# Modulation vectors of a convolution layer, partly from TensorE: eight tiles moved from VectorE into the convolution's last groups and a layer norm, with more room for banded matrices

## The chip, the cores and the metric

One core of a Trainium2 chip runs the whole program in one launch. The metric is device time in microseconds (us); the kernel before took 2941.39 us, the median of three runs (2937.71 to 2943.6). In the text PE is TensorE, DVE is VectorE, ACT is ScalarE, POOL is GpSimd and SP is the engine that issues most of the transfers.

## The reference

Two layers over 1024 latent tokens and 256 context tokens of width 1024. Layer 0 mixes tokens with a convolution module, layer 1 with grouped-query attention; each is followed by a SwiGLU FFN. Only layer 0's convolution matters here:

```python
mod_x = (silu_c @ w_mod[i] + b_mod[i])[:, None, :]
mod_c = silu_cc @ w_mod[i] + b_mod[i]
sh_x, sc_x, g_x, shf_x, scf_x, gf_x = jnp.split(mod_x, N_MOD, axis=-1)
...
u = h @ w_pw1 + b_pw1
a, gt = jnp.split(u, 2, axis=-1)
u = a * jax.nn.sigmoid(gt)
u = lax.conv_general_dilated(u, w_dw[:, None, :], ..., feature_group_count=u.shape[-1]) + b_dw
u = jax.nn.silu(layernorm(u, ln_g, ln_b))
return u @ w_pw2 + b_pw2
```

The modulation vectors are 6 x 1024 numbers for each of two conditions (latents and context). In the kernel they are 48 tiles of 128, with f the tile's number: tiles 0 to 15 are needed first, 16 to 23 scale the mixer's output, 24 to 39 are shift and scale of the FFN's norm, 40 to 47 scale its output.

## The kernel before

The 1280 tokens lie side by side in three pieces: the context C (256), the latents' first half L and second half R (512 each). The channels are on the partitions, eight tiles of 128.

**pw1** (lines 440 to 474) is a loop over k = 0 to 7. Each iteration multiplies two weight tiles (value and gate) with C, L and R in turn, each product in three matmuls (L454, L455, L456: high and low parts). It yields four times a piece, twelve times an iteration. At a piece's end ACT applies the gate's sigmoid (L462) and DVE multiplies (L463), which also empties the two PSUM banks; PE has three banks for pw1, so the third quarter of the next piece waits for that L463. After C's and R's L463 the result is loaded in another layout into U by transfers that SP and ACT issue in turn (L472). One iteration later ACT and DVE split U into a high and a low part (L161, L164).

**The convolution** runs as matmuls with banded matrices, in 64 groups (8 for each k). A group is ten matmuls (L532, L533, L535), ACT's eviction with bias (L536) and DVE's sum (L538). Three PSUM banks rotate, so a group needs the L538 of the group three before it. DVE builds a group's two banded matrices ("a map" is the pair, and each L506 makes one half of it) from a window of the weights (L164 of 320 columns prepares it). The maps lie in places that rotate: three in tile T6 at first; three in T1 and three in T2 are added in the last iteration, so nine. A place is free again when its group has run. The generator of the groups (`cg`) is advanced at the yields of pw1, two of three of them from the yield 22 on; at pw1's end 16 groups are left (48 to 63). After the eight groups of one k, DVE sums them over the channel (L565, L567). While the last eight run, `shift` centres the context's part ahead of its norm: L575 on DVE, L577 on PE, L594 on DVE.

**The modulation** of tiles 0 to 15 is made on PE in the prologue (`mod_pe`, L236 to L250). Tiles 16 to 39 are made on DVE during pw1 (`mod_dve`, L257 to L282): one multiply-and-sum instruction for each of the two conditions and tile (L273, and a short second instruction that reads the sum out), 48 in all, each tile's weights loaded ahead into one of two buffers in turn. The generator `modg` is advanced at two of three yields. The rest (40 to 47) is made later and isn't touched.

**After the groups** come the layer norms: `ln("C")` (L594 and L630 centre, L365 sums over channels, L370 and L343 to L351 compute the root, L379 spreads it, L643 and L646 apply), then `ln("L")`, `pw2("C")` (L665), `ln("R")`, `pw2("L")` and so on. `derive` (L319, L324) turns modulation vectors into columns. What R's norm reads (tile T5) is loaded from DRAM (L610) like C's and L's, piece by piece, as soon as the groups of a k are written.

Within what the buffers and the data allow, a scheduler orders each engine's instructions when the program is built; so where an instruction stands on its engine is not where the code calls it. The rows of that order are shown with the change. The names in them: HR holds the pw1 result and the groups' sums, KB holds U and raw windows, HS the split U, q the windows, T the maps, ps PSUM, cst constants, wr and wl weights.

Of the kernel before, what the change touches and what calls it, by code (L numbers as in the profile page):

```python
# [9 lines left out]
F32R = mybir.dt.float32r  # L10
# [5 lines left out]
P = 128  # L16
D = 1024
KT = D // P
# [20 lines left out]
NM = 5  # L39
# [16 lines left out]
class Kern:  # L56
# [454 lines left out]
    def conv(self):  # L511

        nc, c = self.nc, self.c
        for q in range(KT * CG):
            k, g = divmod(q, CG)
            u2, v = self.u2[k % 2], self.v[k == KT - 1]
            for _ in range(2):
# [1 line left out]
                    self.conv_maps()  # L519
            if q == CG * (KT - 1):  # L520
                self.cvs = {}
                for b, t in (("C", "KB"), ("L", "T4"), ("R", "T5")):
                    self.cvs[b] = self.T(t, [P, KT, PIECES[b][1] - PIECES[b][0]])
                    for j in range(KT - 1):
                        self.load_cv(b, j)
# [13 lines left out]
            if g == CG - 1:  # L539
# [6 lines left out]
                        eng.dma_start(d[k].rearrange("g q n -> q g n"), v[:, :, o0:o0 + nn])  # L546
                if k == KT - 1:
                    self.load_cv("L", k)
                    self.load_cv("R", k)

                self.conv_sum(v[:, CG - 2:] if k == KT - 1 else v, k)
            elif k == KT - 1:
# [638 lines left out]
    def build(self):  # L1191
        nc, a, c = self.nc, self.a, None
# [6 lines left out]
        cr = [hr[:, TOK + nv:TOK + nv + 1024], self.T("HV", [P, 1024])]  # L1199
# [64 lines left out]
        mraw = kt[:, CG * UW + nw:]  # L1264
        q = self.room()
        self.cwin = [q[:, o:o + nw].bitcast(F32R) for o in (0, 512)]
        cw = self.T("T6", [P, 6, NM * P], F32R)
        self.cw = [(cw[:, 2 * i], cw[:, 2 * i + 1]) for i in range(3)]
        self.cwq, self.cwi = [], 0
        for o, n in ((0, 2), (2 + NC_, 2), (UW - 2, 2)):  # L1270
            nc.gpsimd.memset(self.U[:, :, o:o + n], 0.0)
        modg = self.mod_dve(range(16, 40), cr, (mraw, None), self.ps[:, 5:7].rearrange("p a b -> p (a b)"))
        nc.vector.tensor_copy(self.craw[:, 0:1], hs["R"][0][1][:, KT - 1, 0:1].bitcast(F32))
        nc.sync.dma_start(self.craw, a["wwin"][0])
        self.conv_maps()
# [18 lines left out]
        self.banks["st"], self.ring["st"] = [6, 5], 0  # L1294
        for _ in range(4):
# [9 lines left out]
        self.set_banks(mm=[0, 1, 2, 3, 4, 7], st=[5, 6])  # L1305
# [61 lines left out]
        t = self.T("KB", [P, 2, 4, 256], F32R)  # L1367
# [356 lines left out]
```

## Time and profile before

| what | before |
| --- | --- |
| median of three runs | 2941.39 us (2937.71 to 2943.6) |
| the profiled execution, its own time | 2938.98 us |
| its span | 2937.2 us, mean granted PE clock 0.987 |
| prologue | 0 to 60 us |
| pw1 with groups 0 to 47 | 60 to 343 us |
| groups 48 to 63 | 343 to 374 us |
| the context's norm | 374 to 386 us |
| granted PE clock, 375 to 390 us | 0.59 |

Reading it: the page's first part gives each engine's busy time and share of the span. A row of the timeline gives start, duration, engine, line, operation, output and input names with their shapes, and in brackets the idle time before it and what ended it. A table of waits gives for each line what it waited for: us in total, how many times, and the longest. A row of stretches gives busy time and count of each engine, then the granted PE clock, the share of the transfer engines, and GB/s.

### The profile page before, as it was taken

How to read it: one execution, taken by the hardware profiler on the slowest of the kernel's cores; microseconds unless marked ns; L12 is line 12 of the kernel's file. 1: busy time of each engine (PE TensorE's matmuls, PEld its weight loads, DVE VectorE, ACT ScalarE, POOL GpSimd, SP SyncE). 2: the span in 40 equal slices, each digit the busy share in tenths (PEclk: the TensorE clock that was granted, in tenths of full speed). 3: DMA queues.
4: the chain of work that ended last, by engine and by line, in shares of the span. 5: the costliest groups of instructions: out<-in, count | busy, mean ns of one | idle time of the engine just before them, and what ended most of it. 6: DMA issues, size and time to landing. Idle time of an engine off the chain costs nothing.

```text
span 2937.2 us, 42731 instructions
## 1 busy us (share of the span) xinstructions
PE 2847.7 (97%) x16462; PEld 2446.1 (83%) x16462; DVE 2160.7 (74%) x3746; ACT 1335.5 (45%) x2229; POOL 222.6 (8%) x377
## 2 busy tenths in 40 slices
PE   7999989999999999999999999989999999999998
PEld 6888877888888889989888787767777778889997
DVE  6887788847556378877786899786666666786777
ACT  5222255532222245544445688645555543444444
POOL 0000001011022001000011111110000000010000
PEclk9999999999999999999999999999999999999999
DMA  6443444334356224333345211322222143353332
GB/s 249 140 120 98 116 131 145 135 116 143 115 175 198 65 74 165 114 104 112 109 156 170 88 46 46 97 87 81 66 73 83 60 149 99 110 170 104 102 98 75
DMA packets 131755, 336.58 MB, mean 115 GB/s; under 512 B 31328, under 2 KB 52864, under 8 KB 130656
## 3 DMA queue, kind: packets, MB, share of 16 engines
q1 hardware_dynamic: 78016, 222.33, 24.1%
q0 software_dynamic: 29344, 103.83, 10.7%
q10 hardware_dynamic: 24192, 7.70, 1.1%
q8 instruction: 129, 2.11, 0.3%
q14 instruction: 74, 0.61, 0.1%
HBM read 289.50 MB, written 38.93 MB: 112 GB/s over the span
## 4 chain that ended last, share of the span: by engine, by line
PE 86%; DVE 7%; ACT 2%; issue 2%; DMA 2%; ACTq 0%; POOL 0%; SPq 0%; DVEq 0%; POOLq 0%
PE ps L172 15%; PE ps L173 15%; PE ps L174 15%; PE ps L875 4%; PE ps L877 4%; PE ps L876 4%; PE ps L1116 4%; PE ps L1134 4%; PE ps L1140 2%; PE ps L454 2%; PE ps L455 2%; PE ps L456 2%; PE ps L1141 2%; PE ps L185 1%; PE ps L183 1%
## 5 line engine op out<-in xcount | busy, mean ns | idle before, releaser
L172 PE MATMUL ps<-T,wh 128*128 128x512 f32 (+1 forms) x1360 | 502.5, 370 | 1.4 <-ACT T L161 0.8
L174 PE MATMUL ps<-T,wl 128*128 128x512 f32 (+1 forms) x1360 | 500.4, 368 | 2.0 <-DVE wl L148 2.0
L173 PE MATMUL ps<-T,wh 128*128 128x512 f32 (+1 forms) x1312 | 481.4, 367 | 0.2 <-DVE T L164 0.2
L144 ACT CAST wh<-wr 128x1024 fp32r<-128x1024 f32 (+1 forms) x217 | 225.0, 1037 | 419.9 <-PE ps L173 307.2
L148 DVE TENSOR_TENSOR wl<-wr,wh 128x1024 fp32r<-128x1024 f32 (+1 forms) x217 | 261.9, 1207 | 168.5 <-ACT wh L144 167.1
L875 PE MATMUL ps<-T,wh 128*128 128x256 f32 x1092 | 310.7, 285 | 5.0 <-ACT wh L161 4.5
L876 PE MATMUL ps<-T,wh 128*128 128x256 f32 x1092 | 306.5, 281 | 0.0
L877 PE MATMUL ps<-T,wl 128*128 128x256 f32 x1092 | 305.4, 281 | 0.2 <-DVE wl L164 0.2
L1138 DVE TENSOR_TENSOR T<-ps,T 128x512 fp32r<-128x512 f32 x320 | 216.8, 687 | 107.6 <-ACT T L1137 106.8
L172 PEld LDWEIGHTS ps<-T,wh 128*128 128x128 f32 x1360 | 257.8, 190 | 43.7 <-ACT T L1506 1.7
L174 PEld LDWEIGHTS ps<-T,wl 128*128 128x128 f32 x1360 | 257.7, 190 | 42.4 <-DVE wl L148 2.2
L173 PEld LDWEIGHTS ps<-T,wh 128*128 128x128 f32 x1312 | 248.5, 189 | 38.2 <-DVE T L164 1.3
L1137 ACT CAST T<-ps 128x512 fp32r<-128x512 f32 x320 | 186.0, 586 | 191.1 <-PE ps L1134 177.6
L173 PE MATMUL ps<-HS,wh 128*128 128x512 f32 x656 | 257.9, 393 | 0.0
L172 PE MATMUL ps<-HS,wh 128*128 128x512 f32 x608 | 238.4, 392 | 0.9 <-ACT wh L144 0.9
L174 PE MATMUL ps<-HS,wl 128*128 128x512 f32 x608 | 237.5, 391 | 0.0
L875 PEld LDWEIGHTS ps<-T,wh 128*128 128x128 f32 x1092 | 206.1, 189 | 11.2 <-ACT wh L161 6.7
L876 PEld LDWEIGHTS ps<-T,wh 128*128 128x128 f32 x1092 | 206.6, 189 | 0.5
L877 PEld LDWEIGHTS ps<-T,wl 128*128 128x128 f32 x1092 | 206.2, 189 | 0.6 <-DVE wl L164 0.4
L1134 PE MATMUL ps<-cst,T 128*128 128x128 f32 x1100 | 189.6, 275 | 3.2 <-DVE T L1138 3.1
L1122 DVE TENSOR_SCALAR_CACHE_REDUCE T<-ps,rq 128x1280 f32<-128x1280 f32 x110 | 170.0, 1546 | 27.9 <-PE ps L1116 22.1
L1134 PEld LDWEIGHTS ps<-cst,T 128*128 128x128 f32 x1100 | 132.6, 141 | 49.5 <-DVE T L1138 30.8
(377 smaller groups left out, 6195.9 us busy)
## 6 DMA issues: line engine op xcount, KB each, us to landing
wr<-in_w SPq DMA_DIRECT2D x170, 512.0 KB, 3.6
wr<-in_pw SPq DMA_DIRECT2D x35, 512.0 KB, 3.5
HV<-in_wmodT POOLq DMA_DIRECT2D x56, 256.0 KB, 4.1
q<-in_wmodT POOLq DMA_DIRECT2D x56, 256.0 KB, 3.9
KB<-in_w SPq DMA_DIRECT2D x24, 512.0 KB, 3.6
HR<-in_w SPq DMA_DIRECT2D x23, 512.0 KB, 3.7
q<-in_w SPq DMA_DIRECT2D x23, 512.0 KB, 4.2
q<-qsd POOLq DMA_DIRECT2D x32, 256.0 KB, 3.3
```

Of the source, the lines that this page charges most:

```text
L144: nc.scalar.copy(hi, raw)
L148: nc.vector.tensor_tensor(lo, raw, hi.bitcast(F32), op=ALU.subtract)
L172: nc.tensor.matmul(out[:, :n], lhsT=wh, rhs=xh, start=k == 0, stop=False)
L173: nc.tensor.matmul(out[:, :n], lhsT=wh, rhs=xl, start=False, stop=False)
L174: nc.tensor.matmul(out[:, :n], lhsT=wl, rhs=xh, start=False, stop=k == nk - 1)
L875: nc.tensor.matmul(out, lhsT=wh, rhs=bh, start=first and k == 0, stop=False, **skip)
L876: nc.tensor.matmul(out, lhsT=wh, rhs=bl, start=False, stop=False, **skip)
L877: nc.tensor.matmul(out, lhsT=wl, rhs=bh, start=False, stop=k == 3, **skip)
L1122: nc.vector.tensor_scalar(out=pt, in0=sc, scalar1=rq[:, h:h + 1], scalar2=None, op0=ALU.mult, op1=ALU.min, accum_out=mn)
L1134: nc.tensor.transpose(tp[:, h * P:(h + 1) * P], Ps[h][:, j * P:(j + 1) * P], c["ident"])
L1137: nc.scalar.copy(ph, tp)
L1138: nc.vector.tensor_tensor(pl, tp, ph.bitcast(F32), op=ALU.subtract)
```

## The change

- `mod_dve` makes only tiles 16 to 31, on DVE as before; `modg` is advanced at every second yield instead of two of three.
- Tiles 32 to 39 are made by `mod_pe` on PE: eight matmuls of two rows (L242), ACT's copy (L245), a transpose (L247) and ACT's two additions of the bias (L249). Five of them are called between the last groups, three inside `ln("C")`. Their weights (512 KB each) are loaded from the start of the last pw1 iteration on, into the buffers of `mod_dve` and of raw weights, and after pw1 into T5.
- What R's norm reads can no longer go to T5 during the groups: its eight loads (L610) come after `ln("C")`. `derive(0, (1, 2))` moves there too.
- T3 gives three more places for maps (twelve), and the last four yields of pw1 may call `conv_maps` twice, up to as many maps as there are places ahead of the group that runs (`self.cq`).
- The first two weight tiles of pw2 are loaded two groups later.

From line 512 on the conv's lines have numbers greater by one after the change (L532 becomes L533, L538 becomes L539, and so on).

```diff
         for q in range(KT * CG):
+            self.cq = q
...
-                for b, t in (("C", "KB"), ("L", "T4"), ("R", "T5")):
+                for b, t in (("C", "KB"), ("L", "T4")):
...
                 if k == KT - 1:
                     self.load_cv("L", k)
-                    self.load_cv("R", k)
...
-        modg = self.mod_dve(range(16, 40), cr, (mraw, None), self.ps[:, 5:7].rearrange("p a b -> p (a b)"))
+        modg = self.mod_dve(range(16, 32), cr, (mraw, None), self.ps[:, 5:7].rearrange("p a b -> p (a b)"))
...
                 if k == KT - 1 and i >= 8:
-                    if i == 8:
-                        cw = self.T("T2", [P, 6, NM * P], F32R)
+                    for t in ("T3", "T2") if i == 8 else ():
+                        cw = self.T(t, [P, 6, NM * P], F32R)
                         self.more_maps([(cw[:, 2 * j], cw[:, 2 * j + 1]) for j in range(3)])
-                    self.conv_maps()
+                    for _ in range(2):
+                        if len(self.cwq) < self.cq + len(self.cw):
+                            self.conv_maps()
                 if 12 * k + i >= 22 and i % 3 != 1:
                     next(cg)
-                if k and i % 3 != 2:
+                if k and i % 2 == 0:
                     next(modg, None)
+                if k == KT - 1 and i == 0:
+                    for _ in modg:
+                        pass
+                    places = [mraw, self.raw(), self.raw()]
+                    for j in range(3):
+                        nc.sync.dma_start(places[j], a["wmod"][32 + j])
...
+        self.banks["md"], self.ring["md"] = [0, 1, 2], 0
+        t = self.T("T5", [P, 4, 1024])
+        places += [t[:, j] for j in range(4)] + [t[:, 0]]
+        for j in range(3, 7):
+            nc.sync.dma_start(places[j], a["wmod"][32 + j])
+
+        def mod_next():
+            j = self.mj
+            self.mj += 1
+            self.mod_pe(32 + j, places[j])
+            if j == 3:
+                nc.sync.dma_start(places[7], a["wmod"][39])
...
-        self.derive(0, (1, 2))
         for i, _ in enumerate(cg):
+            if i in (0, 1, 2, 6, 8):
+                mod_next()
             if i == 7:
                 self.raws.append(self.room())
-            if i in (2, 4):
-                self.pre.append(self.load_raw(a["pw2"][i // 2 - 1]))
+            if i in (4, 6):
+                self.pre.append(self.load_raw(a["pw2"][i // 2 - 2]))
...
         for b in ("C", "L"):
-            for _ in self.ln(b, tags[b][1], sv[b]):
-                pass
+            for i, _ in enumerate(self.ln(b, tags[b][1], sv[b])):
+                if b == "C" and i in (0, 4, 7):
+                    mod_next()
+            if b == "C":
+                self.cvs["R"] = self.T("T5", [P, KT, 512])
+                for j in range(KT):
+                    self.load_cv("R", j)
+                self.derive(0, (1, 2))
```

Three places on DVE show how the order changes. The first is in pw1's third iteration (k = 2): the last rows up to L's L463 (512 columns), which starts at 139.76 us in the trace before. Rows named ISA are L273, a long one and its short read-out; T is the maps' tile. Before:

```order
L273 ISA ps,mod_101<-KB,HR 128x1024
L273 ISA mod_101 128x1
L273 ISA ps,mod_102<-KB,HV 128x1024
L273 ISA mod_102 128x1
L506 TENSOR_TENSOR T_624<-q,cst 128x640
L538 TENSOR_TENSOR HR<-HR,ps 128x162
L506 TENSOR_TENSOR T_624<-q,cst 128x640
L164 TENSOR_TENSOR q<-KB,q 128x320
L506 TENSOR_TENSOR T_624<-q,cst 128x640
L538 TENSOR_TENSOR HR<-HR,ps 128x162
L506 TENSOR_TENSOR T_624<-q,cst 128x640
L463 SCALAR_TENSOR_TENSOR HR<-ps,cst,sm 128x512
```

The same rows with the change:

```order
L273 ISA ps,mod_102<-KB,HV 128x1024
L273 ISA mod_102 128x1
L164 TENSOR_TENSOR q<-KB,q 128x320
L273 ISA ps,mod_101<-wr_73,HR 128x1024
L273 ISA mod_101 128x1
L273 ISA ps,mod_102<-wr_73,HV 128x1024
L273 ISA mod_102 128x1
L539 TENSOR_TENSOR HR<-HR,ps 128x162
L506 TENSOR_TENSOR T_624<-q,cst 128x640 x2
L273 ISA ps,mod_101<-KB,HR 128x1024
L273 ISA mod_101 128x1
L463 SCALAR_TENSOR_TENSOR HR<-ps,cst,sm 128x512
```

The scheduler has drawn later modulation instructions forward: between C's L463 and this one stand nine instead of five, with the same six halves of maps. The two that stand ahead of L164 (of HS) in this iteration before stand behind it now; in the fourth iteration (k = 3) there are none at all.

The second place is the fifth iteration (k = 4), from L164 of U's split to the context's L463 (256 columns), which starts at 205.72 us in the trace before. Before:

```order
L164 TENSOR_TENSOR HS<-KB,HS 128x1328
L273 ISA ps,mod_101<-wr_74,HR 128x1024
L273 ISA mod_101 128x1
L506 TENSOR_TENSOR T_624<-q,cst 128x640
L538 TENSOR_TENSOR HR<-HR,ps 128x162
L506 TENSOR_TENSOR T_624<-q,cst 128x640
L273 ISA ps,mod_102<-wr_74,HV 128x1024
L273 ISA mod_102 128x1
L463 SCALAR_TENSOR_TENSOR HR<-ps,cst,sm 128x256
```

With the change:

```order
L164 TENSOR_TENSOR HS<-KB,HS 128x1328
L506 TENSOR_TENSOR T_624<-q,cst 128x640
L539 TENSOR_TENSOR HR<-HR,ps 128x162
L506 TENSOR_TENSOR T_624<-q,cst 128x640
L273 ISA ps,mod_101<-KB,HR 128x1024
L273 ISA mod_101 128x1
L463 SCALAR_TENSOR_TENSOR HR<-ps,cst,sm 128x256
```

One modulation instruction stands there instead of two.

The third place is the end of the last iteration (k = 7), up to R's L463, which starts at 343.70 us in the trace before. In both orders five halves (L506 x5) directly follow L's L463 ahead of these rows. Before:

```order
L506 TENSOR_TENSOR T_2701<-q,cst 128x640
L538 TENSOR_TENSOR HR<-HR,ps 128x162
L506 TENSOR_TENSOR T_2701<-q,cst 128x640
L164 TENSOR_TENSOR q<-KB,q 128x320
L506 TENSOR_TENSOR T_2701<-q,cst 128x640
L538 TENSOR_TENSOR HR<-HR,ps 128x162
L506 TENSOR_TENSOR T_2701<-q,cst 128x640
L565 TENSOR_REDUCE sm<-HR 128x162
L567 TENSOR_TENSOR HR<-HR,sm 128x162
L463 SCALAR_TENSOR_TENSOR HR<-ps,cst,sm 128x512
```

With the change (T_2767 is the new tile T3, T_624 is T6, T_2680 is T1):

```order
L506 TENSOR_TENSOR T_2767<-q,cst 128x640
L539 TENSOR_TENSOR HR<-HR,ps 128x162
L506 TENSOR_TENSOR T_2767<-q,cst 128x640 x4
L506 TENSOR_TENSOR T_624<-q,cst 128x640
L164 TENSOR_TENSOR q<-KB,q 128x320
L539 TENSOR_TENSOR HR<-HR,ps 128x162
L506 TENSOR_TENSOR T_624<-q,cst 128x640
L565 TENSOR_REDUCE sm<-HR 128x162
L506 TENSOR_TENSOR T_2680<-q,cst 128x640
L567 TENSOR_TENSOR HR<-HR,sm 128x162
L506 TENSOR_TENSOR T_2680<-q,cst 128x640 x3
L463 SCALAR_TENSOR_TENSOR HR<-ps,cst,sm 128x512
```

Seven more halves stand ahead of R's L463 (16 instead of 9), and one more ahead of L's. Behind R's L463 stand four halves, then two L539; before it was two, then one L538; in all ten halves follow instead of fourteen. Elsewhere: in the context's norm two L319 of `derive` now stand between L370 and L343, and SP's queue has two loads of modulation weights ahead of its last four L472 and two behind, where three L610 and seven L610 stood.

More of the change, by code (lines that the diff above doesn't have):

```diff
@@ L1284, in build @@
                 if k == KT - 1 and i >= 8:
-                    if i == 8:
-                        cw = self.T("T2", [P, 6, NM * P], F32R)
+                    for t in ("T3", "T2") if i == 8 else ():
+                        cw = self.T(t, [P, 6, NM * P], F32R)
                         self.more_maps([(cw[:, 2 * j], cw[:, 2 * j + 1]) for j in range(3)])
-                    self.conv_maps()
+                    for _ in range(2):
+                        if len(self.cwq) < self.cq + len(self.cw):
+                            self.conv_maps()
                 if 12 * k + i >= 22 and i % 3 != 1:
                     next(cg)
-                if k and i % 3 != 2:
+                if k and i % 2 == 0:
                     next(modg, None)
+                if k == KT - 1 and i == 0:
[4 more added lines that the diff above has]
+                        nc.sync.dma_start(places[j], a["wmod"][32 + j])
         nc.scalar.activation(self.tiny([P, 16], "nv")[:, :1], c["ones"], AF.Silu)
         self.banks["st"], self.ring["st"] = [6, 5], 0
+        self.banks["md"], self.ring["md"] = [0, 1, 2], 0
[9 more added lines that the diff above has]
+                nc.sync.dma_start(places[7], a["wmod"][39])
+        self.mj = 0
         for _ in range(4):
@@ L1298, in build @@
             self.split_u(KT - 1, g0, g0 + CG // 2)
-        self.derive(0, (1, 2))
         for i, _ in enumerate(cg):
+            if i in (0, 1, 2, 6, 8):
+                mod_next()
             if i == 7:
                 self.raws.append(self.room())
-            if i in (2, 4):
-                self.pre.append(self.load_raw(a["pw2"][i // 2 - 1]))
-        self.set_banks(mm=[0, 1, 2, 3, 4, 7], st=[5, 6])
+            if i in (4, 6):
+                self.pre.append(self.load_raw(a["pw2"][i // 2 - 2]))
+        self.set_banks(mm=[0, 1, 2, 3, 4, 7], st=[5, 6], md=[7])
         sv, yv, fv = ({b: [] for b in PIECES} for _ in range(3))
```

## Prediction

> **What bounds the kernel now.** I read the page first, then PE's waits, then the stretches, then the timelines of PE and DVE where PE waits.
>
> ```profile
> PE 2847.7 (97%) x16462; PEld 2446.1 (83%) x16462; DVE 2160.7 (74%) x3746; ACT 1335.5 (45%) x2229; POOL 222.6 (8%) x377
> ```
>
> PE is busy for 97% of the span, so only its idle time and its clock can be won or lost. The change lies in the first 400 us; two tables of PE's waits say what ended its idle time there (us in total, times, longest), from 60 to 346 us and from 346 to 430 us:
>
> ```profile
> PE ps L454 <- DVE HR L463: 1.6, 1, 1.6
> ...
> PE ps L577 <- DVE sm L575: 5.9, 2, 3.5
> PE ps L532 <- DVE HR L538: 3.2, 4, 1.6
> ```
>
> All are waits for DVE. The stretches add what a wait costs beyond itself (busy times, then the granted clock):
>
> ```profile
> 200.00:210.00 10.00, 8.37 (x35) 6.79 (x34) 9.33 (x15) 1.57 (x5) 0.00 (x0) 0.85 0.24 64
> 210.00:300.00 90.00, 90.00 (x521) 80.36 (x520) 66.52 (x106) 19.87 (x36) 0.00 (x0) 1.00 0.32 88
> 364.00:375.00 11.00, 10.62 (x66) 10.21 (x66) 8.64 (x24) 5.09 (x14) 0.00 (x0) 0.84 0.43 117
> 375.00:390.00 15.00, 6.37 (x20) 4.95 (x21) 10.70 (x37) 5.33 (x12) 0.00 (x0) 0.59 0.24 73
> ```
>
> Apart from one wait the pw1 stage is bound by PE alone (90.00 of 90.00). The clock falls in the 10 us that hold the wait and in the 11 us behind the wait at L577. A clock of 0.84 over 11 us is half clock for 2 x 0.16 x 11 = 3.5 us, so 1.75 us lost; 0.85 over 10 us is 1.5. This is the wait in pw1, on DVE and then on PE:
>
> ```profile
> 200.26 1.54 DVE L164 TENSOR_TENSOR HS<-KB,HS 128x1328 fp32r<-128x1328 f32 x1 [3.37 <-ACT HS L161]
> ...
> 204.57 1.22 DVE L273 CUSTOM_DVE_ANT_0 ps<-wr,HV 128x1024 f32<-128x1024 f32 x1
> ...
> 205.72 0.48 DVE L463 SCALAR_TENSOR_TENSOR HR<-ps,cst,sm 128x256 f32<-128x256 f32 x1
> ```
> ```profile
> 206.25 0.50 PE L454 MATMUL ps<-T,wh 128*128 128x512 f32 x1 [1.64 <-DVE HR L463]
> ...
> 207.44 0.63 PE L455 MATMUL ps<-T,wh 128*128 128x512 f32 x1
> ```
>
> L463 empties a PSUM bank that PE's next quarter of a piece needs; two modulation instructions stood ahead of it. PE waited 1.64 us, then ran matmuls of 0.63 instead of 0.39 us. So the wait cost 1.6 + about 1.7 = 3.3 us. The Trainium skill (TensorE: Matmul & The Clock Gate, Part 1: The HAM clock gate) has the clock fall after an idle window of some 3.4 us that runs freely; here it fell after 1.64 us idle, so I let the trace decide. By that page's rule the shorter waits below would cost no clock, and the sum would be about 1.7 us lower.
>
> **Part 1: sixteen fewer modulation instructions on DVE in pw1.** Their price is their spacing, and that of a map's half (L506) is a sixth of a row:
>
> ```profile
> 148.14 1.22 DVE L273 CUSTOM_DVE_ANT_0 ps<-wr,HR 128x1024 f32<-128x1024 f32 x1
> ...
> 149.45 1.23 DVE L273 CUSTOM_DVE_ANT_0 ps<-wr,HV 128x1024 f32<-128x1024 f32 x1
> ```
> ```profile
> 330.74 4.49 DVE L506 TENSOR_TENSOR T<-q,cst 128x640 fp32r<-128x640 f32 x6
> ```
>
> That is 1.31 us and 0.74 us. 16 x 1.31 = 21 us leave DVE, but beside PE's work: worth nothing where PE is bound, worth the whole 3.3 us where PE waits. In the fifth iteration (k = 4) the order of the change has one modulation instruction rather than two between L164 and that L463, and none rather than three ahead of the L463 that lets L164's data be loaded. L463 would come over 1.31 us earlier, so I count this wait as gone: -3.3.
>
> But the others now bunch. In the third iteration (k = 2) nine of them, not five, stand between the context's L463 and that of L:
>
> ```profile
> 121.91 1.54 DVE L164 TENSOR_TENSOR HS<-KB,HS 128x1328 fp32r<-128x1328 f32 x1 [0.65 <-ACT HS L161]
> ...
> 125.07 0.48 DVE L463 SCALAR_TENSOR_TENSOR HR<-ps,cst,sm 128x256 f32<-128x256 f32 x1
> ...
> 129.77 0.32 DVE L538 TENSOR_TENSOR HR<-HR,ps 128x162 f32<-128x162 f32 x1 [1.61 <-ACT HR L536]
> ...
> 139.76 0.74 DVE L463 SCALAR_TENSOR_TENSOR HR<-ps,cst,sm 128x512 f32<-128x512 f32 x1
> ```
> ```profile
> 143.09 0.40 PE L454 MATMUL ps<-T,wh 128*128 128x512 f32 x1
> ```
>
> PE needs L463's bank for the third quarter of piece R, at 143.09. Before, L463 ended at 140.5, 2.6 us early. Now: two modulation instructions stand behind L164 that stood ahead of it, which puts the context's L463 at some 127.0 (126.5 to 127.7); from there nine of 1.31, six halves of 0.74, and 1.5 for L463 itself, three L538 and the small L164 make 17.7, so L463 starts at 144.7 and ends at 145.4. The waits of 1.61 and 0.5 for ACT that DVE had in this stretch are filled. PE waits 145.4 - 143.1 = 2.3 us, and half a clock behind it costs 1.7: +4.0. The bounds are nothing (if PE is that much late by then anyway) and 6. Part 1 together: +0.7, from -3.3 to +2.7.
>
> **Part 2: two maps a step and three more places.** The last iteration's order puts 16 halves, not 9, between L's L463 and R's, and one more ahead of L's:
>
> ```profile
> 329.33 0.83 DVE L506 TENSOR_TENSOR T<-q,cst 128x640 fp32r<-128x640 f32 x1 [1.13 <-PE ps L456]
> ...
> 343.70 0.75 DVE L463 SCALAR_TENSOR_TENSOR HR<-ps,cst,sm 128x512 f32<-128x512 f32 x1 [1.81 <-ACT sm L462]
> 344.37 1.55 DVE L506 TENSOR_TENSOR T<-q,cst 128x640 fp32r<-128x640 f32 x2
> 348.07 0.32 DVE L538 TENSOR_TENSOR HR<-HR,ps 128x162 f32<-128x162 f32 x1 [2.16 <-ACT HR L536]
> ```
> ```profile
> 348.45 0.41 PE L532 MATMUL ps<-HS,T 128*128 128x324 f32 x1 [1.61 <-DVE HR L538]
> ```
>
> Eight halves are 5.9 us, of which idle time (1.81, and 0.8 of small gaps) hides 2.6: R's L463 starts 3.3 us later, at 347.0. Four halves follow it, not two, ahead of L538: 347.0 + 0.67 + 4 x 0.74 = 350.6. Group 51 needs that L538's bank, so PE starts it at 350.9, not 348.45: its wait is 4.1, not 1.61. The loads of U, which wait for R's L463, slip by the same 3.3 us, and ACT, whose queue issues half of them, holds its evictions (L537 now) behind them till about 350.
>
> What is won for it: 10 halves follow R's L463, not 14, and the wait ahead of the first L577:
>
> ```profile
> 363.48 0.42 DVE L575 TENSOR_TENSOR sm<-part,cst 128x256 f32<-128x256 f32 x1
> ```
> ```profile
> 363.96 1.13 PE L577 MATMUL ps<-sm,cst 128*128 128x256 f32 x2 [3.48 <-DVE sm L575]
> ...
> 371.85 0.31 PE L532 MATMUL ps<-HS,T 128*128 128x324 f32 x1
> ...
> 373.15 0.31 PE L532 MATMUL ps<-HS,T 128*128 128x324 f32 x1
> ...
> 374.27 0.35 PE L535 MATMUL ps<-HS,T 128*128 128x324 f32 x1
> ```
>
> **Part 3: five modulation tiles between the groups.** Their price is in the prologue's rows, one of 16 matmuls and the groups of the transpose and of ACT's copy:
>
> ```profile
> 16.15 1.91 PE L242 MATMUL ps<-KB,cs 128*2 128x128 f32 x16
> L247 PE MATMUL ps<-cst,sm 2*128 2x2 f32 x16 | 3.5, 218 | 1.5 <-ACT sm L245 1.3 <-DMA HS<-in_xT 0.2
> L245 ACT COPY sm<-ps 2x128 f32<-2x128 f32 x16 | 4.0, 249 | 14.7 <-PE ps L242 14.7
> ```
>
> 8 x 0.119 + 0.11 = 1.06 us a tile, 5.3 for five, wholly on PE. The conv's end, from 350.9: 13 groups (51 to 63) of 1.30, the spacing of the last two groups at 371.85 and 373.15, are 16.9; five tiles 5.3; L577 0.6; the wait for L575, now only a group and a half of tiles behind the last L538 it needs, 1.3; one wait for L245 0.4; half a clock behind the wait of 4.1, 1.7 as at 364. Last group's end 350.9 + 26.2 = 377.1, against 374.4 (L535 at 374.27 and its 0.18 us of PE): +2.7. It is +1.0 without the clock's loss, +4.4 if the loads of U hold up L164 and L537 by 1.7 more.
>
> **Part 4: three tiles in the context's norm, derive and the loads moved.**
>
> ```profile
> 381.85 0.15 DVE L370 TENSOR_SCALAR nv<-ps 128x2 f32<-128x2 f32 x1
> 382.03 0.17 DVE L343 TENSOR_SCALAR nq<-nv 128x2 int32<-128x2 int32 x1
> ```
> ```profile
> 386.02 2.93 PE L665 MATMUL ps<-T,wr 128*128 128x256 f32 x6 [1.11 <-ACT T L646]
> ```
>
> PE idles there, so tiles 5 and 6 cost nothing. Tile 7 stands ahead of L365, and two instructions of derive (0.15 each like L370) that need tile 7's last ACT result now stand between L370 and L343. At full clock tile 7 and its copies are done as L365's sums are; at the half clock that the stretch 375 to 390 shows a tile takes 2.1 us. I take +0.5, from -0.4 to +1.5. R's loads (eight of 256 KB) move behind this on SP's queue, to about 382. R's norm comes after L's, and that begins to centre its piece only at 390.69:
>
> ```profile
> 390.69 1.88 DVE L630 TENSOR_TENSOR T<-T,ps 128x512 f32<-128x512 f32 x3 [2.52 <-PE ps L603]
> ```
> ```profile
> 346.00:358.00 12.00, 8.67 (x58) 7.52 (x57) 9.93 (x18) 4.18 (x10) 0.00 (x0) 1.00 0.91 265
> ```
>
> Their 2 MB take some 8 us at the 265 GB/s moved from 346 to 358, and lie under that; without the cover they would cost those 8 us. The four loads of modulation weights stand where L's and R's did in SP's queue; they go with part 2's upper bound. The raw buffers rotate by two in the FFN stages: the page's only sizeable wait there is
>
> ```profile
> L875 PE MATMUL ps<-T,wh 128*128 128x256 f32 x1092 | 310.7, 285 | 5.0 <-ACT wh L161 4.5
> ```
>
> so I bound that by 1.5 us either way, and take 0. How pw2's start falls into the half-clock time adds another 1.5 either way.
>
> **The sum.** +0.7 + 2.7 + 0.5 = +3.9 us. The profiled execution took 2938.98 us (span 2937.2), 2.4 below the median of the three runs, so 2942.9 for it and 2945.3 on the median. A measurement of this kernel can tell about 0.2%, 5.9 us, from no change.
>
> **Rivals.** *DVE's relief wins.* The bunch at k = 2 meets a PE that is late already, and U's loads are ready as before; then -3.3, the conv's end at -0.9, the norm -0.4: -4.6, or 2936.8. For it: DVE ends with 21 us less work and every wait is DVE's. Against: the order puts the work ahead of the very L463s. Chance 0.2, half of it beyond 0.2%.
>
> *The two late L463s cost more (slower).* Loads of weights hold up the bunch at k = 2 (wait 4, and 1.2 more at k = 1, where four stand ahead of L's L463), U's loads land late (+4.4), tile 7 runs at half clock (+1.5): part 1 becomes 4 + 1.2 + 1.7 - 3.3 = +3.6, and the whole 3.6 + 4.4 + 1.5 = +9.5; hardly all at once, so I put it at +8, 2949.4. It decides once the two waits together exceed 8.5 us rather than 6.4. For it: the clock fell after each wait over 1.64 us. Chance 0.28.
>
> *It does nothing:* PE stays bound in pw1 and the tail pays back what it gains: 0, 2941.4. Chance 0.1. My forecast has 0.42.
>
> **The numbers.** Faster by over 0.2%: half the first rival, 0.1. Slower: most of the second and a tail of the forecast, 0.25 + 0.06 = 0.31. Same: 0.59. The range 2938.5 to 2951 leaves out half of the first rival and the tail of the second.
>
> **What would show it.** Right: PE's wait on L463 between 60 and 346 us moves to 140 to 150 with 2 to 3 us; L532's successor waits 3.5 to 4.5 us near 347 to 351; L577's first wait is under 2; the last group ends 3 to 4 us later. Wrong: no wait of PE between 60 and 346 us, or group 51 on time; then the first rival holds.

## The result and the profile after

The change makes the kernel slower. Its runs have a median of 2956.28 us; one of the four was disturbed (4016.31 us at a granted clock of 0.651), the three others run from 2954.47 to 2957.09 with a median of 2955.46. The kernel before has 2940.55 beside them. The ratio is 1.0052, with an interval from 1.0039 to 1.0065, so +15.3 us (11.5 to 19). The forecast of 2945.3 and its whole range (up to 2951.0) lie below it. Below, "us by the ratio" is (ratio - 1) x 2940.

The profiled execution of the change took 2957.09 us (span 2955.3), against 2938.98 before. The page's first part:

```profile
PE 2872.1 (97%) x16598; PEld 2459.9 (83%) x16598; DVE 2142.7 (73%) x3714; ACT 1340.3 (45%) x2253; POOL 222.6 (8%) x377
```

DVE has 18 us less to do, PE 24 us more. PE's records grow by 136: eight transposes, and 128 for eight tiles, that is 16 a tile. The waits of PE, from 60 to 346 us and from 340 to 440 us (us in total, times, longest):

```profile
PE ps L454 <- DVE HR L463: 2.9, 1, 2.9
...
PE ps L533 <- DVE HR L539: 4.2, 1, 4.2
PE ps L379 <- DVE nr L351: 2.7, 1, 2.7
PE ps L665 <- ACT T L646: 1.1, 1, 1.1
PE ps L247 <- ACT sm L245: 0.7, 2, 0.4
PE ps L242 <- ACT mod L249: 0.5, 1, 0.5
```

With the rows of 0.2 us that are left out here, the waits from 340 to 440 us come to 9.6 us; the same view of the kernel before adds up to 16.0. So PE waits less there than before, and neither wait at L577 is left. What there is now is work; the stretches show it (busy times of PE, PEld, DVE, ACT, POOL, then granted clock, DMA share, GB/s):

```profile
120.00:160.00 40.00, 37.05 (x216) 32.92 (x215) 36.59 (x57) 8.52 (x16) 0.00 (x0) 1.00 0.46 140
346.00:360.00 14.00, 9.76 (x55) 9.53 (x55) 13.45 (x23) 3.50 (x8) 0.00 (x0) 0.76 0.85 267
360.00:380.00 20.00, 20.00 (x134) 14.08 (x132) 11.64 (x27) 6.93 (x24) 0.00 (x0) 1.00 0.67 198
380.00:400.00 20.00, 16.44 (x109) 10.55 (x109) 9.09 (x34) 6.28 (x21) 0.00 (x0) 0.99 0.31 95
```

From 360 to 380 us PE is busy throughout, at full clock. PE's timeline through the changed stretch, from the wait in pw1 to pw2's start:

```profile
148.43 0.50 PE L454 MATMUL ps<-T,wh 128*128 128x512 f32 x1 [2.94 <-DVE HR L463]
...
353.00 0.64 PE L533 MATMUL ps<-HS,T 128*128 128x324 f32 x1 [4.24 <-DVE HR L539]
...
359.52 0.31 PE L533 MATMUL ps<-HS,T 128*128 128x324 f32 x1
...
371.30 0.59 PE L577 MATMUL ps<-sm,cst 128*128 128x256 f32 x2
...
376.39 0.24 PE L534 MATMUL ps<-HS,T 128*128 128x162 f32 x1
376.47 0.34 PE L533 MATMUL ps<-HS,T 128*128 128x324 f32 x1
...
377.48 0.38 PE L242 MATMUL ps<-T,cs 128*2 128x128 f32 x2
377.79 0.34 PE L534 MATMUL ps<-HS,T 128*128 128x162 f32 x1
378.06 0.38 PE L242 MATMUL ps<-T,cs 128*2 128x128 f32 x2
...
388.60 0.35 PE L536 MATMUL ps<-HS,T 128*128 128x324 f32 x1
388.88 0.22 PE L247 MATMUL ps<-cst,sm 2*128 2x2 f32 x1
389.03 1.91 PE L242 MATMUL ps<-T,cs 128*2 128x128 f32 x16
...
395.08 1.91 PE L242 MATMUL ps<-T,cs 128*2 128x128 f32 x16 [0.50 <-ACT mod L249]
396.92 0.60 PE L365 MATMUL ps<-cst,acc 128*128 128x1 f32 x4
...
402.23 1.22 PE L665 MATMUL ps<-T,wr 128*128 128x256 f32 x2 [1.11 <-ACT T L646]
```

At 389.03 one tile stands by itself, between two transposes: 16 records, 1.91 us. Each of a tile's eight matmuls leaves two records. At 377 the scheduler has put a tile's matmuls one by one between those of a group. There L534 and one matmul of the tile (two records) take 378.06 - 377.48 = 0.58 us; without a tile L534 holds PE for 376.47 - 376.39 = 0.08, so the tile's matmul takes 0.50, not 1.91 / 8 = 0.24. Of the 40 matmuls of the five tiles 18 stand alone in this way; 18 x 0.26 = 4.7 us. PE's weight loads show an idle time before each return to the group:

```profile
377.78 0.19 PEld L534 LDWEIGHTS ps<-HS,T 128*128 128x128 f32 x1 [0.22 <-issue]
```

From 359.52 to the last group's end (388.60 + 0.18 = 388.78) are 29.26 us. Ten groups of 1.30 are 13.0, L577 is 0.24 (371.30 to 371.54, the next start); 16.0 are left for five tiles with four transposes: 3.2 us a tile. The part of PE's groups by line from 359.52 to 388.8 us confirms the count (80 records, five tiles):

```profile
L242 PE MATMUL ps<-T,cs 128*2 128x128 f32 x32 | 5.8, 272 | 0.0
L242 PE MATMUL ps<-wr,cs 128*2 128x128 f32 x32 | 4.6, 272 | 0.0
L242 PE MATMUL ps<-KB,cs 128*2 128x128 f32 x16 | 2.2, 272 | 0.0
```

DVE at k = 2, at pw1's end and in the norm:

```profile
147.63 0.75 DVE L463 SCALAR_TENSOR_TENSOR HR<-ps,cst,sm 128x512 f32<-128x512 f32 x1
...
348.51 0.75 DVE L463 SCALAR_TENSOR_TENSOR HR<-ps,cst,sm 128x512 f32<-128x512 f32 x1
349.18 3.03 DVE L506 TENSOR_TENSOR T<-q,cst 128x640 fp32r<-128x640 f32 x4
352.62 0.61 DVE L539 TENSOR_TENSOR HR<-HR,ps 128x162 f32<-128x162 f32 x2 [0.41 <-ACT HR L537]
...
397.56 0.16 DVE L370 TENSOR_SCALAR nv<-ps 128x2 f32<-128x2 f32 x1 [1.28 <-PE ps L365]
398.00 0.32 DVE L319 SCALAR_TENSOR_TENSOR col<-mod,cst 128x8 f32<-128x8 f32 x2 [0.28 <-ACT mod L249]
```

Four halves stand between R's L463 and L539, and L370 waits for L365, which stands behind the last tile.

Three marks divide the stretch: the start of pw1's last matmul (L456), of the last group's last matmul, and of the first L665. They are 342.55, 374.27 and 386.02 us before, 344.47, 388.60 and 402.23 after. So pw1 ends 1.9 us later, the conv's end grows by 12.4 us (31.72 to 44.13), the context's norm by 1.9 (11.75 to 13.63); together 16.2. The rest of the span differs by 1.9.

### The profile page after: what moved, and what is told of

It is laid out like the page before. It is cut to its first block, busy times and chain, and to the rows that moved or that the text cites. A ratio compares the mean times of both kernels' runs of the same rounds, so it can differ in the third digit from the quotient of the medians.

```text
span 2955.3 us, 42993 instructions
## 1 busy us (share of the span) xinstructions
PE 2872.1 (97%) x16598; PEld 2459.9 (83%) x16598; DVE 2142.7 (73%) x3714; ACT 1340.3 (45%) x2253; POOL 222.6 (8%) x377
## 3 DMA queue, kind: packets, MB, share of 16 engines
q0 software_dynamic: 29344, 103.83, 10.7%
## 4 chain that ended last, share of the span: by engine, by line
PE 59%; DVE 5%; ACT 2%; issue 1%; DMA 0%; POOL 0%; DVEq 0%; ACTq 0%; POOLq 0%
PE ps L172 10%; PE ps L173 10%; PE ps L174 10%; PE ps L875 4%; PE ps L877 4%; PE ps L876 4%; PE ps L1116 4%; PE ps L1134 4%; PE ps L1140 2%; PE ps L1141 2%; PE ps L185 1%; PE ps L184 1%; PE ps L183 1%; DVE T L1138 1%; PE ps L1015 1%
## 5 line engine op out<-in xcount | busy, mean ns | idle before, releaser
L148 DVE TENSOR_TENSOR wl<-wr,wh 128x1024 fp32r<-128x1024 f32 (+1 forms) x222 | 268.3, 1209 | 186.4 <-ACT wh L144 184.9
```

Of the source, the lines that this page charges most:

```text
L148: nc.vector.tensor_tensor(lo, raw, hi.bitcast(F32), op=ALU.subtract)
```

## The experiments

Theory A: the price is PE's work for the tiles. Theory B: the price is the two late L463s, at k = 2 and at pw1's end, with the clock that falls behind them. This table gives all kernels by the same marks ("conv's end" and "norm" are the two distances between them), each from one profiled execution, and the ratio to the kernel before on the same chip. From pw2's start on, where hardly anything of the experiments' edits reaches, the profiled executions take between 2546.6 us (e6) and 2554.5 us (e10); so a sum of marks and a ratio can differ by several us:

| kernel | ratio (interval) | us by the ratio | pw1's end | conv's end | norm |
| --- | --- | --- | --- | --- | --- |
| before | | | 342.55 | 31.72 | 11.75 |
| the change | 1.0052 (1.0039 to 1.0065) | +15.3 | 344.47 | 44.13 | 13.63 |
| e1_one_of_eight | 1.0015 (1.0006 to 1.0024) | +4.4 | 347.40 | 33.86 | 12.70 |
| e2_no_tiles | 1.0009 (1.0 to 1.0018) | +2.6 | 343.73 | 32.34 | 11.85 |
| e3_nine_places | 1.0044 (1.0031 to 1.0056) | +12.9 | 345.20 | 41.56 | 13.63 |
| e4_ring_alone | 0.9997 (0.9988 to 1.0006) | -0.9 | 340.42 | 31.91 | 11.76 |
| e5_tiles_twice | 1.0105 (1.009 to 1.0121) | +30.9 | 344.30 | 60.63 | 17.31 |
| e6_all_in_norm | 1.0041 (1.0029 to 1.0054) | +12.1 | 345.09 | 31.27 | 29.45 |
| e8_cadence | 0.9985 (0.9976 to 0.9994) | -4.4 | 340.78 | 32.22 | 11.84 |
| e9_spread | 0.9996 (0.9987 to 1.0005) | -1.2 | 341.41 | 32.75 | 11.76 |
| e10_rounded | 1.0046 (1.0033 to 1.0058) | +13.5 | 346.72 | 37.07 | 13.17 |
| e11_tiles_alone | 1.0022 (1.0013 to 1.0032) | +6.5 | 342.10 | 40.65 | 13.62 |
| e12_together | 1.0053 (1.004 to 1.0065) | +15.6 | 349.94 | 41.93 | 13.48 |
| e13_together_cadence | 1.0049 (1.0035 to 1.0063) | +14.4 | 344.32 | 38.94 | 14.93 |

**e1_one_of_eight**: the tiles 32 to 39 get the first of their eight matmuls only; the rest of their sums is left out.

```diff
-            for k in range(KT):
+            for k in range(nk):
...
-            self.mod_pe(32 + j, places[j])
+            self.mod_pe(32 + j, places[j], nk=1)
```

> The change with only the first of the eight matmuls of each of the tiles 32 to 39; seven eighths of their sum are left out, everything else (loads, copies, transposes, order on DVE) stays. Theory A, PE's work for the tiles is the cost (16 matmul records of 0.119 us each, not 8): 14 records go from each tile, 8 x 14 x 0.119 = 13.3 us of PE; some 2 us come back as the wait for L575 that the tiles hid, so 2943 to 2947 us. Theory B, the two late L463 and the clock behind them are the cost: they stay, so the time falls by 3 us at most, 2953 or more.

Measured 2944.21 us, as A has it. Seven eighths of the tiles' matmuls cost 15.3 - 4.4 = 10.9 us, with both late L463s still there (its wait at k = 2 was 4.7 us, the one at L533 4.2).

**e2_no_tiles**: tiles 32 to 39 with their loads and copies are left out, their columns set to zero.

```diff
+        for s in range(2):
+            nc.gpsimd.memset(self.mod[0][s][:, 32:40], 0.0)
...
-            self.mod_pe(32 + j, places[j])
```

> The change without the tiles 32 to 39 at all: no loads, matmuls, copies or transposes for them, their modulation columns are zero. DVE's order in pw1 and the twelve places stay as in the change. Theory A: 8 x 2.1 us of PE go, 2 us of waits come back: 2940 to 2944 us, that is, DVE's relief alone gains nothing against the kernel before. Theory B: the late L463 remain with their waits, so still slower than before by 8 us or more: 2949 or more.

Measured 2942.77 us. Its waits are those of B, almost whole:

```profile
PE ps L454 <- DVE HR L463: 2.3, 1, 2.3
...
PE ps L533 <- DVE HR L539: 5.0, 3, 4.3
PE ps L577 <- DVE sm L575: 4.8, 2, 2.4
```

All that B names is in this kernel, and it is 2.6 us slower than before, not 15.3. The tiles, with their loads and copies, cost the other 12.7; in the marks 44.13 - 32.34 + 13.63 - 11.85 = 13.6. B falls as the main cause. The two waits at L577 are back: in the change the tiles fill them.

**e3_nine_places**: the change without T3's three places and without the second map in a step.

```diff
-                    for t in ("T3", "T2") if i == 8 else ():
-                        cw = self.T(t, [P, 6, NM * P], F32R)
+                    if i == 8:
+                        cw = self.T("T2", [P, 6, NM * P], F32R)
...
-                    for _ in range(2):
-                        if len(self.cwq) < self.cq + len(self.cw):
-                            self.conv_maps()
+                    self.conv_maps()
```

> The change without T3's three places and with one map a step, as before; tiles on PE as in the change. R's last L463 then has 9 halves of maps ahead of it, not 16, and comes when ACT's sigmoid is done. Theory A: group 51 starts some 2.6 us earlier and keeps its clock, but the tiles' 16 us stay: 2952 to 2956 us. Theory B: most of the loss at the conv's end goes with the wait of 4.2 us: 2948 or less.

Measured 2952.4 us. PE's longest wait at L533 is 1.7 us in place of 4.24, and the conv's end is 2.6 us shorter. On the ratios the 2.4 us between the two kernels lie inside the intervals: likely, not settled.

**e4_ring_alone**: the kernel before with nothing but the three places and the two maps a step.

```diff
-                    if i == 8:
-                        cw = self.T("T2", [P, 6, NM * P], F32R)
+                    for t in ("T3", "T2") if i == 8 else ():
+                        cw = self.T(t, [P, 6, NM * P], F32R)
...
-                    self.conv_maps()
+                    for _ in range(2):
+                        if len(self.cwq) < self.cq + len(self.cw):
+                            self.conv_maps()
```

> The kernel before with T3's three places and two maps a step alone; all 24 tiles on DVE, none on PE. Theory A: group 51 waits 4 us rather than 1.6 and loses the clock behind it, the wait for the first L577 falls from 3.5 to 2 or less: -1 to +3 us against before. Theory B: the late L463 costs as it does in the change, so 5 us or more slower than before.

Measured 2938.36 us, no difference. Its waits after 346 us:

```profile
PE ps L578 <- DVE sm L576: 4.8, 2, 2.4
PE ps L533 <- DVE HR L539: 4.2, 1, 4.2
```

The wait at group 51 is as long as in the change, but the waits for the shift are 1.1 us shorter than before (4.8, not 5.9): the places move a wait. Its pw1 has the modulation of before and no wait on L463 at all; the one of 1.64 us in the profile before comes in some executions only. DVE's order around it is the same in both: before, the L164 ahead of it waited 3.37 us for ACT's half of the split, here 1.48, and L463 came in time.

**e5_tiles_twice**: each tile's eight matmuls are made a second time, into columns that nobody reads.

```diff
+            for k in range(KT if twice else 0):
+                nc.tensor.matmul(out[0:2, 2 * P:3 * P], lhsT=self.cs[:, k, :], rhs=raw[:, k * P:(k + 1) * P],
+                                 start=k == 0, stop=k == KT - 1)
```

> The change with the eight matmuls of each of the tiles 32 to 39 made a second time into other columns of the same bank, whose result isn't used. Theory A, PE's work of 16 records of 0.119 us a tile is the cost: 8 x 1.91 = 15.3 us more, of which a little lies in the norm's idle time: 2966 to 2972 us. If the tiles cost through what waits for them (copies, banks, loads) and not through PE's time, the second set lies beside that: under 2962.

Measured 2971.95 us: eight times eight matmuls more cost 30.9 - 15.3 = 15.6 us, 1.95 a tile. By the marks it is 16.5 us for the five in the conv's end (3.3 each) and 3.7 for the three in the norm (1.2 each), 20.2 in all; behind pw2's start this execution is 6.1 us shorter than the change's. A part of that is the clock: pw2's first six matmuls take 1.56 us here and 2.93 in the change, where they ran at a granted clock of 0.50. A tile's price is its matmuls.

**e6_all_in_norm**: all eight are made in the context's norm, none between groups. (Tiles 33 and 34 read pw2's weights here, since those are loaded into their buffers first.)

```diff
-            if i in (0, 1, 2, 6, 8):
-                mod_next()
...
-                if b == "C" and i in (0, 4, 7):
+                if b == "C" and i < 8:
```

> The change with all eight tiles inside the context's norm, none between the groups. If PE's idle time in the norm (about 8 us before) can take tiles, five more there cost less than their 10.5 us between the groups: 2948 to 2952 us. If each tile there stands ahead of a matmul on the norm's chain (L577, L365), nothing is won: 2954 to 2958.

Measured 2954.19 us: the norm is no free place. Its PE timeline:

```profile
394.53 1.91 PE L242 MATMUL ps<-T,cs 128*2 128x128 f32 x16 [0.50 <-ACT mod L249]
396.37 0.61 PE L365 MATMUL ps<-cst,acc 128*128 128x1 f32 x4
...
397.63 1.91 PE L242 MATMUL ps<-T,cs 128*2 128x128 f32 x16 [0.50 <-ACT mod L249]
399.94 0.22 PE L247 MATMUL ps<-cst,sm 2*128 2x2 f32 x1 [0.40 <-ACT sm L245]
400.66 1.91 PE L242 MATMUL ps<-T,cs 128*2 128x128 f32 x16 [0.50 <-ACT mod L249]
```

One PSUM bank serves the tiles, so each waits for ACT to have copied and added the one before: 3.0 to 3.1 us from tile to tile. The conv's end is as short as without tiles (31.27), the norm 17.6 us longer.

**e8_cadence**: e2_no_tiles with `modg` advanced as before; the columns of tiles 32 to 39 are zero.

```diff
-                if k and i % 2 == 0:
+                if k and i % 3 != 2:
```

> The change without the tiles 32 to 39, as in the run without tiles (2942.8 us), but with the old rule for advancing the modulation generator (two of three yields instead of one of two). The order then has five modulation instructions, not nine, between the context's L463 and L's in the third iteration, and none ahead of the fifth iteration's L463. If the bunch's wait of 2.9 us costs its length: 2939 to 2940.5 us, with no wait of PE on L463 in pw1. If it is hidden: 2942 or more.

Measured 2937.04 us: 7.0 us by the ratio under e2_no_tiles, whose only difference is the cadence, and the intervals do not overlap. No wait on L463 is left in its pw1. The -4.4 against the kernel before is not DVE's relief alone: the eight tiles and their loads are left out altogether, and the twelve places are in. Against e4_ring_alone, which has the places and all of DVE's work, the 3.5 us lie inside the intervals, and the profiled e8 starts pw2 at 384.84 us, e4 at 384.09; so that the relief gains time is not shown. For the cadence the marks point the same way as the ratio, with about half the size: with the new cadence pw1 ends at 345.9 on the mean of eight kernels (the change, e1, e2, e3, e5, e6, e10, e12), with the old one at 342.0 on the mean of five (before, e4, e8, e11, e13): 3.8 us.

**e9_spread**: e4_ring_alone with `modg` advanced at eight of twelve yields, spread differently. (One buffer of its modulation weights is reloaded too early, so one tile is computed from other weights.)

```diff
-                if k and i % 3 != 2:
+                if k and i in (0, 2, 3, 5, 6, 8, 9, 11):
```

> The kernel before with the twelve places and two maps a step (2938.4 us alone), all 24 tiles on DVE, and the modulation generator advanced at yields 0, 2, 3, 5, 6, 8, 9 and 11 of an iteration: 48 instructions over six iterations, with at most one of them ahead of R's L463 and none between L164 and the context's L463. If the wait of 1.6 us at 204 us and the clock behind it are worth 3.3 us and go: 2934 to 2936 us, faster than before by 4 to 6. If they come back elsewhere: 2938 or more.

Measured 2939.47 us, a miss: the wait that it was to remove was not there in e4_ring_alone either.

**e10_rounded**: POOL rounds the tiles' weights to the reduced float32 that the groups use, and the vector with them; the low bits are lost.

```diff
+        if fast:
+            hi = self.wp.tile([P, 1024], F32R, tag="wh", name="wh")
+            nc.gpsimd.tensor_copy(hi, raw)
+            raw = hi
```

> The change with the weights of tiles 32 to 39 first rounded by POOL into the reduced format that the convolution's matmuls read (POOL's copies are new; the modulation loses the low bits), so that a tile's eight matmuls are eight records, not sixteen. Theory A, PE's time by passes and columns: if a record of 128 columns takes a quarter of the 0.227 us that pw1's 512 columns are apart, 0.06 us, a tile takes 0.6 us and 8 x 1.4 = 11 us go: 2944 to 2947 us. If only the number of records halves at 0.119 us each: 2948 to 2950. Theory B, the number of stops between groups, copies and waits: unchanged, 2954 or more.

Measured 2953.32 us, a miss. The tiles do get cheap on PE, 8 records and 0.64 us, and one that stands alone between a group's matmuls stays cheap (378.98 to 379.04):

```profile
378.98 0.22 PE L249 MATMUL ps<-wh,csr 128*2 128x128 f32 x1
379.04 0.29 PE L541 MATMUL ps<-HS,T 128*128 128x162 f32 x1
...
384.22 0.64 PE L249 MATMUL ps<-wh,csr 128*2 128x128 f32 x8
```

The conv's end shortens by 7.1 us, to 37.07. But pw1 ended 2.3 us later in its profile, and waits stand where the tiles' matmuls did:

```profile
PE ps L540 <- DVE HR L546: 6.3, 2, 4.8
PE ps L254 <- ACT sm L252: 3.0, 3, 1.9
...
PE ps L584 <- DVE sm L582: 2.1, 2, 1.1
```

At pw2's start it is 5.3 us ahead of the change, in the span 3.8, by the ratio 1.8. Less work on PE is not time while waits for DVE and ACT take its place. Why the ratio shows only 1.8 of the 5.3 us was not found.

**e11_tiles_alone**: the change with the cadence and the nine places of before.

```diff
-                    for t in ("T3", "T2") if i == 8 else ():
...
+                    self.conv_maps()
...
-                if k and i % 2 == 0:
+                if k and i % 3 != 2:
```

> The change with the old rule for advancing the modulation generator and with nine places and one map a step, so the tiles on PE without the bunch of modulation instructions and without the maps ahead of R's last L463. If the parts add up (5.7 us for the bunch, by the runs without tiles; 3.9 us for the places, by the run with nine): 2956.3 - 9.6 = 2946.7, so 2945 to 2949 us, and what is left over the kernel before, 5 to 9 us, is the tiles less DVE's relief. If the two waits overlap or return elsewhere: 2951 or more.

Measured 2946.94 us, as the addition of parts had it. Against e8_cadence, which also has the twelve places, the tiles cost 10.9 us by the ratio; conv's end and norm give 40.65 - 32.22 + 13.62 - 11.84 = 10.2.

**e12_together**: a priority keeps a tile's matmuls together, so that none stands alone between those of a group.

```diff
-        with self.later(20):
+        with self.later(20 if together is None else together):
...
-            self.mod_pe(32 + j, places[j])
+            self.mod_pe(32 + j, places[j], together=-2000)
```

> The change with each tile's eight matmuls ahead of the groups' matmuls in the scheduler's order instead of behind them, so that a tile's stand together (three tiles between groups 48 and 49, two together later) and don't alternate with the matmuls of a group. If each change between the two kinds costs PE time, as the change's trace suggests (3.2 us a tile between groups against 1.9 together, so 1.1 more than with its transpose), 5 x 1.1 = 5.5 us go; three tiles (6.2 us) ahead of group 51 fill its wait of 4.2 us: 2956.3 - 5.5 - 4.2 = 2946.6, so 2945 to 2949. If only the passes cost and alternating is free, the wait's filling alone: 2951 to 2953.

Measured 2954.62 us, a miss. The scheduler now puts two tiles (32 records) right behind pw1's end, where their PSUM banks still hold R's last quarter:

```profile
351.12 1.03 PE L242 MATMUL ps<-wr,cs 128*2 128x128 f32 x8 [0.29 <-ACT sm L462]
354.18 2.78 PE L242 MATMUL ps<-wr,cs 128*2 128x128 f32 x24 [2.02 <-DVE HR L463]
...
382.60 0.41 PE L533 MATMUL ps<-HS,T 128*128 128x324 f32 x1 [1.66 <-DVE HR L539]
...
383.68 0.55 PE L533 MATMUL ps<-HS,T 128*128 128x324 f32 x1
```

A tile does take 16 records of 0.116 us here (2.78 / 24), and the conv's end is 2.2 us shorter than in the change, not 5.7 (five times 3.2 less 1.91 and a transpose of 0.15). PE's waits in it came out 1.0 us longer: 2.0 and 0.3 new at L242, 1.3 less at L533. And behind the wait at 382.60 the granted clock was 0.58 in one microsecond and 0.50 from 384 to 390 us: half clock for 6.8 us, so 3.4 lost, where the change lost 2.6 behind group 51's wait. Of the missing 3.5 us that leaves 1.7 not placed.

**e13_together_cadence**: e12_together with the old cadence.

```diff
-                if k and i % 2 == 0:
+                if k and i % 3 != 2:
```

> The run with the tiles' matmuls together, and the old rule for advancing the modulation generator, so no bunch of nine in the third iteration. If the parts add up, 5.7 us less than that run: 2940 to 2943, about the kernel before. If the bunch's wait is filled in another way: 2945 or more.

Measured 2950.8 us, a miss too. The 24 records behind the wait took 4.45 us, not 2.78; the granted clock was 0.50 from 350 to 352 us:

```profile
348.56 4.45 PE L242 MATMUL ps<-wr,cs 128*2 128x128 f32 x24 [2.02 <-DVE HR L463]
```

The ratio is inside that of e12_together, so it adds nothing on the cadence.

Put together by the ratios: the change without tiles and cadence -4.4 (e8), the cadence +7.0 (e2 against e8), the tiles +12.7 (the change against e2). The three add up to 15.3 because each starts where the one before ends; the sum proves nothing. The tiles by the other pair (e11 against e8) are +10.9. By their intervals these figures are uncertain by 3 to 5 us.

## Why the prediction was wrong, point by point

**The failed step** is the tile's price in part 3, "8 x 0.119 + 0.11 = 1.06 us a tile, 5.3 for five". The row "16.15 1.91 PE L242 MATMUL ps<-KB,cs 128*2 128x128 f32 x16" was read as two tiles of eight matmuls. It is one: a float32 matmul leaves two records. The profile before held the check: for the prologue's 16 tiles the row of L247 that the prediction quotes counts 16 transposes, and L242 there counts:

```profile
L242 PE MATMUL ps<-T,cs 128*2 128x128 f32 x192 | 24.2, 283 | 9.6 <-DMA T<-in_wmod 9.4
L242 PE MATMUL ps<-KB,cs 128*2 128x128 f32 x64 | 7.6, 273 | 0.1
```

That is 256 records for 128 matmuls. By itself a tile is 1.91 + 0.15 for its transpose = 2.06 us, 10.3 for five; 5.0 us of the miss are this. The other 5.7 come from the place: between a group's matmuls five tiles took 16.0 us, and the 18 matmuls that stand alone account for 4.7 of the 5.7 (0.26 more each). The prediction took the tiles as standing together, which nothing in the prologue's rows could show for this place, and it gave no upper bound for it. With 16.0 in place of 5.3 the sum is 3.9 + 10.7 = +14.6, against 15.3 measured. That it comes so near is partly luck, since other terms missed too and offset each other: by the marks pw1 is +1.9 where the sum has +0.7, the conv's end +12.4 where it has 2.7 + 10.7 = 13.4, the norm +1.9 where it has +0.5.

**Part 1** had the right mechanism. The wait on L463 went to 148.43 us, forecast 140 to 150; it is 2.94 us, forecast 2.3. L463 started at 147.63, not 144.7, and PE reached it at 145.5, not 143.1: both late by about the same. The granted clock did not fall there (1.00 from 120 to 160 us), so the 1.7 us put down for it were not lost in this execution; in those with a longer wait some were (below). The gain of 3.3 at k = 4 was no gain of the change's: e4_ring_alone has the old cadence and no such wait. pw1's end came 1.9 us later; over many profiles the new cadence costs 3.8. The forecast of +0.7 was too low.

**Part 2** was right in its order and in its sizes: group 51 waited 4.24 us (forecast 4.1) and started 353.00 (350.9, and 1.9 of the 2.1 are pw1's). Behind it three groups took 359.52 - 353.00 = 6.52 us in place of 3.9: the granted clock was 0.50 from 352 to 358 us, which cost 2.6, forecast 1.7. The first L577 waited for nothing (forecast 1.3).

**Part 4** was wrong in "tiles 5 and 6 cost nothing": one PSUM bank serves the norm's tiles, so tile 7 waited 0.50 us for ACT's L249 of tile 6 and began at 395.08; L365 starts at 396.92 only behind it, L370 waited 1.28 us for it, and L319 0.28 more. The norm cost +1.9, above the bound of +1.5; the half clock was not the cause (0.99 from 380 to 400 us). e6_all_in_norm shows the mechanism five tiles longer. From pw2's start on the two spans differ by 1.9 us, which is within what that part varies by from run to run; the move of R's loads shows no cost beyond it.

**The rivals.** "The two late L463s cost more" came nearest in time and was wrong in its cause: with both of them and no tiles the kernel loses 2.6 us, and the two waits together came to 2.94 + 4.24 = 7.2 us, not over 8.5. "DVE's relief wins" was not in play here; e8_cadence, the change without its tiles and its cadence, is 4.4 us faster than before, but, as said there, that the relief did it is not shown. No rival had PE's own work as the price: the prediction opens with "only its idle time and its clock can be won or lost", and work added to PE is neither.

**What stays open.** How much of the alternation's 5.7 us a better place would give back was not isolated, since e12_together also moved the tiles, its waits and its half clock. Nor is it known why a tile's matmul that stands alone takes 0.50 us. pw1's end varies by several us among kernels of one cadence (343.7 to 349.9 with the new one); the clock, below, is part of it.

## What to carry to other kernels

Before an instruction is priced from a row, count its records against something whose number is known, here the transposes: a float32 matmul leaves two. Work that moves from an engine with slack to the one that is 97% busy costs its duration less the waits that it fills (here the 4.8 us at L577), and more where a scheduler puts it piece by piece between other matmuls; that needs a row of alternating matmuls as its upper bound. Relief on the engine with slack is worth no more than the waits for it were, and a new cadence can bunch the same work ahead of the one instruction that is waited for.

## What the runs showed of the hardware

**Float32 matmuls.** 128 columns with two rows out took 0.24 us (two records, 1.91 / 8), and 0.08 us (one record, 0.64 / 8) once both operands were rounded: three times. That the two records come from one matmul, e1_one_of_eight shows: with one matmul a tile L242 leaves 16 records for eight tiles. The Trainium skill (FP8 and Floating Point Precision, TensorE Precision Notes) has true float32 as four passes through the array; four times the rounded row would be 0.32 us, an estimate that the trace does not reach; four times the 0.06 us of the rounded matmul that stands alone in e10 (378.98 to 379.04) would be 0.24. No run here counts the passes; the records show two.

**Alternating the two kinds.** A float32 matmul between two rounded ones took 0.50 us in place of 0.24, with 0.22 us in which the next weight load waited for issue. A rounded one between the same matmuls shows no such price: in e10 L541 follows it after 0.06 us.

**The clock behind a wait.** In the eight kernels with the bunch at k = 2 the granted clock from 120 to 160 us was 1.00 where PE's wait was 2.3, 2.3 or 2.94 us (e2, e6, the change), and 0.96 where it was 3.1, 3.4, 3.7, 3.8 or 4.7 (e5, e3, e10, e12, e1). The Trainium skill (TensorE: Matmul & The Clock Gate, Part 1: The HAM clock gate) puts the fall after an idle window of about 3.4 us that runs freely. These eight nearly agree with it; the fall after 1.64 us at 206 us in the profile before does not, so a wait's length alone did not decide it. Nor do e12 and e13: both wait 2.02 us ahead of the same 24 records, which then take 2.78 us in one and 4.45 in the other.
